# RWKV's small products on the undivided TensorE array, with a re-ordered start and end, in a hybrid decode step

## Chip, cores and metric

The kernel runs on one core of a Trainium2 chip. The metric is the device time of one execution in microseconds (us), taken as the median of several runs. PE is TensorE (matmuls; PEld its weight loads), DVE is VectorE, ACT is ScalarE, POOL is GpSimd, SP issues the DMAs.

## What is computed

One decoder layer over T = 304 tokens: 16 meta tokens and a prompt of 256, and 8 sequences of 4 sampled tokens. Two head groups stand side by side: RWKV-7 (16 heads of 64) and retention (4 heads of 256). Cut to what matters:

```python
xn = rms_norm(x, norm_mix); z = xn @ w_in            # 2048 -> 3360 + 4096 columns
z_a, z_b = z[..., :RWKV_COLS], z[..., RWKV_COLS:]
zs = z_a + mu * (z_prev - z_a)                        # token shift; then r, k, v, decay, a, gate
# rwkv7_scan, per token and head (S is 64x64):
sa = S @ a_t
S = S * w_t + outer(sa, b_t) + outer(v_t, k_t)
out_t = S @ r_t
# retention: (q k^T * decay mask) v, and a 256x256 state for each head
h = x + concat(o_a, o_b) @ w_out
h = h + (silu(hn @ w_gate) * (hn @ w_up)) @ w_down    # hn = rms_norm(h), d_ff = 5632
y = rms_norm(h, norm_final)                           # and all the states
```

## The kernel before

**Main stream.** All weights lie in HBM as one stream in the order in which they are used. `Step.main` takes them in tiles of up to 128 output columns; a tile of the input projection is 16 blocks of 128 rows. `load` brings 1,024 columns by DMA (`wr`), `halve` splits 512 of them into a rounded part on ACT (`wh`) and the rest on DVE (`wl`), and each block takes three matmuls (`xh,wh`, `xl,wh`, `xh,wl`) in fp32r into an accumulator `acc` in PSUM. Two accumulators take turns. `evacuate` scales the finished tile by 1/rms (`rstd1`); while that is not known, ACT copies the raw accumulator away so that the next tile may go on.

**Small products.** Eight pairs of RWKV heads (two heads of 64 = 128 partitions), each a generator `pair` with `by_token`, `inverse`, `units` and `sample`, work in five units of up to 64 tokens. Four retention heads follow in `ret`. Their matmuls are plain fp32, go to PSUM tiles named `mm`, and read tiles of one scratch arena (`arena_dt.float`). In the pairs most have 64 rows or 64 columns: the two heads stand in the two halves of the array, so products run two at a time on a divided array. `pairmm` is one of these, and the loop of `units` issues them step by step, with an ACT copy between two steps.

**Order.** A planner (`Plan`) writes the order of each engine while the kernel is built: it books a duration for each instruction, and as soon as no generator is ready by its clock, it lets the main stream emit one block. A generator's step that is about to use a divided array yields `DIV`; `Plan.pick` holds such a step back until the array is divided already, two of them wait, or `HOLD` = 2000 ns are over. Each engine's queue is then followed in order on the chip.

**Start.** `start` loads x in five chunks with halves of the weight tiles between, converts all 16 blocks (`xh` on ACT, `xl` on DVE), and `constants` squares x, adds the squares up on POOL, and sums over partitions with eight matmuls against a tile of ones (`ssq`).

**End.** The last tiles of the down projection add into `ht`; ACT squares, DVE adds to `ssq3`, `rstd_from` sums with three matmuls against ones, computes 1/rms on DVE and spreads it with three more matmuls; eight multiplies and DMAs end the kernel.

Of the kernel before, what the change touches and what calls it, by code (L numbers as in the profile page):

```python
# [15 lines left out]
P = 128  # L16
D = 2048
KT = D // P
SEQ = 256
# [22 lines left out]
LATE = 20000  # L42
WR = 4
# [7 lines left out]
HOLD = 2000  # L51

DIV = "div"
# [15 lines left out]
for _n, _w in [("id", 128), ("blk", 128), ("mar", 128), ("i64", 64), ("lvl", 2 * 64), ("m16", 64), ("i16", 16), ("h16", 32), ("h32", 64), ("rst", TP),   # L69
               ("bm64", 8), ("bm128", 8), ("ks", 12), ("kss", 4), ("qs", 128), ("own", 256), ("sel", 32)]:  # L70
    CV[_n] = _o
    _o += _w
# [48 lines left out]

def extent(key):

    if key[0] == "down":
        return min(FSTEP, FT - key[1]), P
    return 8 if key[0] == "out" else KT, 32 if key == ("in", 2) else P


def constants():
# [9 lines left out]
    put("mar", np.concatenate([(s < t), (s <= t)], 1).astype(f))  # L139
    put("i64", (s == t).astype(f))  # L140
# [8 lines left out]
    put("h32", (s // 32 == q // 32).astype(f))  # L149
# [6 lines left out]
    put("bm64", ((r[:64, None] % 32) // 4 == np.arange(8)[None, :]).astype(f))  # L156
# [34 lines left out]
def pack(x_prompt, x_sample, state_shift, state_rwkv, state_ret, meta_tokens, norm_mix, w_in,  # L191
# [20 lines left out]
    for k in seq:  # L212
        m = pick[k[0]](*k[1:])
        n = math.prod(extent(k))
        big[:, at:at + n] = m.reshape(m.shape[0] // P, P, m.shape[1]).transpose(1, 0, 2).reshape(P, n)
        at += n
# [82 lines left out]
class Plan:  # L299
# [57 lines left out]
    def add(self, gen, rank, ready=None):  # L357
        self.made += 1
        self.streams.append([rank, self.made, self.clock["PE"] if ready is None else ready, gen, None])
# [12 lines left out]

    def step(self, s):
        self.ready, self.end = s[2], s[2]
        try:
            s[4] = next(s[3])
# [96 lines left out]
class Step:  # L473
# [79 lines left out]
    def main(self, jobs):  # L553
# [3 lines left out]
        for j in jobs:  # L557
            while self.live == ACC or j.need is not None and not j.need():
                yield False
            self.flush()  # L560
            if j.prep is not None:
                j.prep()
            K, m = extent(j.key)
            n = j.cols[1] - j.cols[0]
            acc = self.t([P, 512], "acc", pool=self.ap_)
            self.live += 1
            for k in range(K):
                o = at % 512
                if o == 0:
                    while self.loaded < min(total, at + WR * WCOLS):  # L570
                        self.load()
                    while self.halved < min(total, at + (WS - 1) * 512):
                        self.halve()
                    hi, lo = self.halves.pop(0)
                xh, xl = (v[:, j.cols[0]:j.cols[1]] for v in j.xs[k])
                self.pe.matmul(acc[:m, :n], hi[:, o:o + m], xh, start=k == 0, stop=False)
                self.pe.matmul(acc[:m, :n], hi[:, o:o + m], xl, start=False, stop=False)
                self.pe.matmul(acc[:m, :n], lo[:, o:o + m], xh, start=False, stop=k == K - 1)
                at += m
                if k < K - 1:  # L580
                    yield True
            self.plan.add(self.evacuate(j, acc), 0, self.plan.clock["PE"] + 250)
            yield True

    def evacuate(self, j, acc):

        if j.ready is not None and j.ready not in self.done:
# [4 lines left out]
            self.live -= 1  # L592
# [7 lines left out]
        self.live -= 1  # L600
# [1027 lines left out]
```

## Time and profile before

| what | value |
|---|---|
| runs | 1596.07, 1601.77, 1598.37 us; median 1598.37 |
| profiled execution | 1596.75 us by the clock, 1594.9 us span |
| PE busy | 1561.5 us (98%), 12336 matmul records |
| PEld / DVE / ACT / POOL busy | 94% / 71% / 52% / 11% |
| chain that ended last | PE `acc` 81%, PE `mm` 10%, DVE arena 2%, POOL arena 1%, waits for x by DMA 1% |
| DMA | 252.55 MB, mean 158 GB/s, 51.2% of the engines' time |

The span is cut by the program into: the start up to about 27 us, the input projection with all small products up to about 650 us, the output projection and the feed-forward part up to 1580 us, and the end. In the third stretch PE takes one `acc` matmul of 288 columns after the other, 133 ns apart. A row of a timeline gives the start in us, the duration, engine, line, operation, tiles, rows*columns of the weights and the output's shape; matmuls are pipelined, so a product's share of PE is read from start to start, not from its duration. An fp32 product appears as two matmul records, an fp32 transpose or an fp32r matmul as one. The line is always that of a helper, so one goes by tiles.

### The profile page before, as it was taken

How to read it: one execution, taken by the hardware profiler on the slowest of the kernel's cores; microseconds unless marked ns; L12 is line 12 of the kernel's file. 1: busy time of each engine (PE TensorE's matmuls, PEld its weight loads, DVE VectorE, ACT ScalarE, POOL GpSimd, SP SyncE). 2: the span in 40 equal slices, each digit the busy share in tenths (PEclk: the TensorE clock that was granted, in tenths of full speed). 3: DMA queues.
4: the chain of work that ended last, by engine and by line, in shares of the span. 5: the costliest groups of instructions: out<-in, count | busy, mean ns of one | idle time of the engine just before them, and what ended most of it. 6: DMA issues, size and time to landing. Idle time of an engine off the chain costs nothing.

```text
span 1594.9 us, 32785 instructions
## 1 busy us (share of the span) xinstructions
PE 1561.5 (98%) x12336; PEld 1492.1 (94%) x12336; DVE 1130.3 (71%) x2603; ACT 833.4 (52%) x1801; POOL 173.3 (11%) x507
## 2 busy tenths in 40 slices
PE   7999999999999999999999999999999999999996
PEld 6998889888998888999999999999999999999996
DVE  5978889887898687777565656566666656565657
ACT  4665666767575656455444444444444444444445
POOL 3343224413143000000000000000000000000000
PEclk9999999999999999999999999999999999999998
DMA  6444343334543456755555555555555555555553
GB/s 236 146 137 127 90 131 114 121 118 156 166 134 118 158 164 220 251 164 160 170 162 170 161 170 161 171 161 170 161 170 162 170 162 170 163 168 163 168 163 109
DMA packets 76142, 252.55 MB, mean 158 GB/s; under 512 B 9296, under 2 KB 14288, under 8 KB 75984
## 3 DMA queue, kind: packets, MB, share of 16 engines
q1 hardware_dynamic: 75984, 250.46, 51.2%
q8 instruction: 97, 1.59, 0.4%
q14 instruction: 61, 0.50, 0.1%
HBM read 236.14 MB, written 14.28 MB: 157 GB/s over the span
## 4 chain that ended last, share of the span: by engine, by line
PE 91%; DVE 3%; POOL 1%; issue 1%; DMA 1%; ACT 1%; SPq 0%; DVEq 0%; ACTq 0%; POOLq 0%
PE acc L294 81%; PE mm L294 10%; DVE arena_dt.float L294 2%; POOL arena_dt.float L294 1%; DVE wl L294 1%; DMA arena_dt.float<-xT 1%; ACT arena_dt.float L294 1%; DMA arena_dt.float<-s0r 1%; ACT wh L294 0%; DVE xl L294 0%; ACT arena_dt.float32r L294 0%; SPq L294 0%; ACT xh L294 0%; POOL shout L294 0%; DVE arena_dt.float32r L294 0%
## 5 line engine op out<-in xcount | busy, mean ns | idle before, releaser
L294 ACT CAST wh<-wr 128x512 fp32r<-128x512 f32 x826 | 510.6, 620 | 596.1 <-PE acc L294 554.8
L294 PE MATMUL acc<-xh,wh 128*128 128x288 f32 (+3 forms) x2608 | 799.2, 306 | 7.5 <-ACT wh L294 6.0
L294 PE MATMUL acc<-xh,wl 128*128 128x288 f32 (+3 forms) x2608 | 777.5, 298 | 1.0 <-DVE wl L294 0.9
L294 PE MATMUL acc<-xl,wh 128*128 128x288 f32 (+3 forms) x2608 | 775.6, 297 | 0.0
L294 DVE TENSOR_TENSOR wl<-wr,wh 128x512 fp32r<-128x512 f32 x826 | 570.4, 692 | 275.6 <-ACT wh L294 251.8
L294 PEld LDWEIGHTS acc<-xh,wh 128*128 128x128 f32 (+1 forms) x2608 | 492.8, 189 | 21.7 <-ACT wh L294 7.6
L294 PEld LDWEIGHTS acc<-xl,wh 128*128 128x128 f32 (+1 forms) x2608 | 494.4, 190 | 3.6 <-issue 0.3
L294 PEld LDWEIGHTS acc<-xh,wl 128*128 128x128 f32 (+1 forms) x2608 | 491.4, 188 | 3.7 <-DVE wl L294 2.4
L294 PE MATMUL acc<-arena_dt.float32r,wh 128*128 128x288 f32 x1408 | 282.3, 295 | 0.3 <-DVE arena_dt.float L294 0.3
L294 PEld LDWEIGHTS acc<-arena_dt.float32r,wh 128*128 128x128 f32 x1408 | 228.2, 190 | 0.8 <-DVE arena_dt.float L294 0.5
L294 PE MATMUL acc<-arena_dt.float32r,wl 128*128 128x288 f32 x704 | 209.6, 298 | 0.0
L294 DVE TENSOR_TENSOR arena_dt.float<-arena_dt.float 128x288 f32<-128x288 f32 (+8 forms) x470 | 150.9, 347 | 13.4 <-PE mm L294 7.7
L294 PE MATMUL mm<-arena_dt.float 64*64 64x64 f32 (+8 forms) x1984 | 141.0, 259 | 7.6 <-DVE arena_dt.float L294 4.3
L294 PEld LDWEIGHTS mm<-arena_dt.float 64*64 64x64 f32 (+4 forms) x1984 | 102.9, 142 | 44.7 <-issue 22.6
L294 DVE TENSOR_TENSOR arena_dt.float<-arena_dt.float,acc 128x288 f32<-128x288 f32 x208 | 94.3, 454 | 65.1 <-PE acc L294 61.7
L294 PEld LDWEIGHTS acc<-arena_dt.float32r,wl 128*128 128x128 f32 x704 | 132.4, 188 | 0.0
L294 ACT COPY arena_dt.float<-mm 128x64 f32<-128x64 f32 (+9 forms) x305 | 85.9, 288 | 61.7 <-PE mm L294 54.5
L294 POOL TENSOR_TENSOR arena_dt.float<-arena_dt.float 128x75 f32<-128x75 f32 (+15 forms) x244 | 93.2, 382 | 94.8 <-DVE arena_dt.float L294 61.3
L294 DVE TENSOR_TENSOR arena_dt.float<-acc,arena_dt.float 128x288 f32<-128x288 f32 (+3 forms) x183 | 73.4, 418 | 33.0 <-PE acc L294 32.4
L294 ACT ACTIVATE arena_dt.float<-arena_dt.float 128x288 f32<-128x288 f32 (+5 forms) x199 | 83.3, 424 | 24.4 <-DVE arena_dt.float L294 21.9
L294 POOL COPY arena_dt.float<-arena_dt.float 128x32 f32<-128x32 f32 (+5 forms) x123 | 45.5, 383 | 216.3 <-DVE arena_dt.float L294 94.8
L294 ACT COPY arena_dt.float<-arena_dt.float 64x16 f32<-64x16 f32 (+4 forms) x128 | 36.5, 313 | 20.0 <-DVE arena_dt.float L294 13.4
(55 smaller groups left out, 638.3 us busy)
## 6 DMA issues: line engine op xcount, KB each, us to landing
wr<-big SPq DMA_DIRECT2D x411, 512.0 KB, 3.6
arena_dt.float<-s0r SPq DMA_DIRECT2D x16, 512.0 KB, 4.4
out_rts<-arena_dt.float SPq DMA_DIRECT2D x16, 512.0 KB, 3.4
arena_dt.float<-xT SPq DMA_DIRECT2D x4, 576.0 KB, 5.4
out_y<-arena_dt.float SPq DMA_DIRECT2D x8, 288.0 KB, 2.4
arena_dt.float<-s0w SPq DMA_DIRECT2D x8, 256.0 KB, 2.7
arena_dt.float<-lora SPq DMA_DIRECT2D x16, 128.0 KB, 2.2
out_rws<-arena_dt.float SPq DMA_DIRECT2D x8, 256.0 KB, 2.7
```

The source lines that it names most:

```text
L294: return f(*a, **k)
```

## The change

1. Each pair's products use the whole array. Operands of two heads are put side by side or on a diagonal with zeros (`arp`, `bku`, `tn`, `yy`, `rh`, `bt`), so that one product of 128 rows and 128 weight columns takes the place of two to four smaller ones. The second level of `inverse` gets its operand by a DVE transpose of the first level's result and no longer by a third set of matmuls. `DIV`, `HOLD` and the choice in `Plan.pick` go.
2. `steps()` orders the weights so that the first two tiles take turns, block by block. `start` brings x one or two blocks at a time, `convert` makes `xh`, `xl` just ahead of the block, and the first tile accumulates in a spare `mm` tile.
3. Ten matmuls of ones with ones stand ahead of the first block (`WARM`), and twice four at the end (`BRIDGE`).
4. All four squares of x are ACT's (two were DVE's), the adds DVE's (they were POOL's), and one of eight `ssq` matmuls is left.
5. At the end DVE squares the last tile, and `rstd_from` adds that square by a second matmul in each column instead of a DVE add.

```diff
+WARM = 10
+BRIDGE = 4
-HOLD = 2000
-DIV = "div"
+def steps():
+    seq = sequence()
+    first = [(key, k) for k in range(KT) for key in seq[:2]]
+    return first + [(key, k) for key in seq[2:] for k in range(extent(key)[0])]
     def pick(self, now):
-        ready = [s for s in self.streams if s[2] <= now]
-        div = [s for s in ready if s[4]]
-        rest = [s for s in ready if not s[4]]
-        if div and (self.mode not in (None, (P, P)) or len(div) > 1 and not rest
-                    or now - min(s[2] for s in div) >= HOLD):
-            return div[0]
-        return rest[0] if rest else None
+        return next((s for s in self.streams if s[2] <= now), None)
     ...
     def start(self):
+        x = lambda a, b: self.sp.dma_start(xr[:, a:b], I["xT"][:, a:b, :])
+        x(0, 1)
+        self.sp.dma_start(self.pvt, I["pv"])
+        self.load(2)
+        for k in range(1, KT, 2):
+            x(k, min(k + 2, KT))
+            if k + 1 < KT:
+                self.load(2)
+        pt = self.ps()
+        for _ in range(WARM):
+            self.pe.matmul(pt[:, :P], self.ones, self.ones, start=True, stop=True)
     ...
     def constants(self):
-            self.pool.tensor_add(xr[:, g:g + 2], xr[:, g:g + 2], xr[:, g + 2:g + 4])
+            self.act.activation(xr[:, g:g + 4], xr[:, g:g + 4], AF.Square)
+            if g % 8:
+                self.dve.tensor_add(xr[:, g - 4:g], xr[:, g - 4:g], xr[:, g:g + 4])
-        for g in range(0, KT, 4):
-            for j in range(2):
-                self.pe.matmul(ssq[:, :T], self.ones, xr[:, g + j, :], start=g + j == 0, stop=g + j == 13)
+        self.pe.matmul(ssq[:, :T], self.ones, xr[:, 0, :], start=True, stop=True)
     ...
     def inverse(self, mt, other):
-                    pe.matmul(pt[h, u * 64:(u + 1) * 64], lhs[h, u, :], rhs[h, u, :], start=True, stop=True)
+                pe.matmul(pt[:, u * P:(u + 1) * P], two(ems[li], u), flat(tn, u), start=True, stop=True)
     ...
     def units(self, p, sc, bkt, sv, sav, tt, arp, dl, o, other):
-            for hi, h in enumerate(HALF):
-                pe.matmul(pt[h, :64], sc[:, hi, u, :64], sv[:, hi, u, :], start=True, stop=True)
+            pe.matmul(pt[:, :P], sc[:, u, 0].rearrange("p h c -> p (h c)"), flat(sv, u), start=True, stop=True)
-            for pt, h in zip(pts, HALF):
-                pe.matmul(pt[h, :64], tt[h, u, :], rh[h], start=True, stop=True)
-            yield
+            pe.matmul(pt[:, :P], two(tt, u), rh.rearrange("p h c -> p (h c)"), start=True, stop=True)
     ...
     def rstd_from(self, ssq, more=None):
+            if more is not None:
+                self.pe.matmul(ps[:n, c:c + 1], more[:, c * n:(c + 1) * n], self.ones[:, :1], start=False, stop=True)
+        if more is not None:
+            self.bridge()
```

Counted along the two programs, the pairs' products and the array's shape change like this (an fp32 product is one here, two records in the trace):

| weights rows*columns, columns moved | before | after |
|---|---|---|
| 64*64, 64 | 464 | 0 |
| 128*64, 64 | 224 | 0 |
| 64*128, 128 | 80 | 0 |
| 128*64, 20 | 64 | 0 |
| 64*64, 512, or 128*128, 512 | 16 | 8 |
| transposes: 64*128, 64 and 128*64, 128 and 128*128, 128 | 80 and 56 and 48 | 0 and 0 and 120 |
| 128*128, 256 | 40 | 72 |
| 128*128, 128 (without those of ones) | 0 | 256 |
| 128*128, 64 and 40 | 0 | 64 and 32 |
| fp32r of 312 columns: half height, full height | 16, 16 | 0, 32 |
| changes of the array's shape, all told | 353 | 12 |

The order on PE at the start, before: the first tile (`acc_144`) is finished, then come the products with ones (`mm_336`), then the second tile (`acc_209`).

```order
L294 MATMUL acc_144<-xh_72,wh_94 128x304
L294 MATMUL acc_144<-xl_73,wh_94 128x304
L294 MATMUL acc_144<-xh_72,wl_95 128x304
...
L294 MATMUL acc_144<-xl_73,wh_130 128x304
L294 MATMUL acc_144<-xh_72,wl_131 128x304
L294 MATMUL mm_336<-arena_dt.float_70,ones_75 128x304 x5
L294 MATMUL acc_209<-xh_72,wh_175 128x290
```

And now: ones first, then the first tile (`mm_111`) and the second (`acc_125`) in turns; the single product with ones for the sum of squares (`mm_390`) stands in the fourth tile.

```order
L300 MATMUL mm_100<-ones_75 128x128 x10
L300 MATMUL mm_111<-xh_72,wh_114 128x304
L300 MATMUL mm_111<-xl_73,wh_114 128x304
L300 MATMUL acc_125<-xh_72,wh_114 128x290
L300 MATMUL acc_125<-xl_73,wh_114 128x290
L300 MATMUL mm_111<-xh_72,wl_115 128x304
L300 MATMUL acc_125<-xh_72,wl_115 128x290
...
L300 MATMUL acc_357<-xh_72,wl_299 128x304
L300 MATMUL mm_390<-arena_dt.float_70,ones_75 128x304
L300 MATMUL acc_357<-xh_72,wh_298 128x304
```

The second tile has moved ahead of the end of the first, and the sum of squares from between the first two tiles to 70 matmuls behind them.

On PE in the first pairs, before (`mm_1646` and `mm_1665` are steps of two inverses, one row for each head and unit):

```order
L294 MATMUL acc_1604<-xh_72,wl_1560 128x288
L294 MATMUL mm_1646<-arena_dt.float_70 64x64
L294 MATMUL mm_1647<-arena_dt.float_70 64x64
...
L294 MATMUL mm_1660<-cst_140,arena_dt.float_70 64x128 x2
L294 MATMUL mm_1665<-arena_dt.float_70 64x64
L294 MATMUL mm_1666<-arena_dt.float_70 64x64
...
L294 MATMUL acc_1604<-xh_72,wh_1559 128x288
```

And now (`mm_1602` and `mm_1631` are steps of one inverse, `mm_1640` transposes of `by_token`):

```order
L300 MATMUL acc_1590<-xh_72,wl_1527 128x288
L300 MATMUL mm_1602<-arena_dt.float_70 128x128 x4
L300 MATMUL acc_1590<-xh_72,wh_1526 128x288
...
L300 MATMUL acc_1590<-xh_72,wl_1557 128x288
L300 MATMUL mm_1631<-arena_dt.float_70 128x64 x4
L300 MATMUL mm_1640<-cst_262,arena_dt.float_70 128x128 x3
L300 MATMUL acc_1590<-xh_72,wh_1556 128x288
```

Steps of several pairs that stood together in one group are now apart, each between matmuls of the main stream: 185 groups of `mm` products have become 242.

On PE at the end, before (`mm_19529` sums over partitions, `mm_19542` spreads 1/rms):

```order
L294 MATMUL acc_19485<-arena_dt.float32r,wl_19445 128x288
...
L294 MATMUL acc_19506<-arena_dt.float32r,wh_19465 128x288 x2
L294 MATMUL acc_19506<-arena_dt.float32r,wl_19466 128x288
L294 MATMUL mm_19529<-ones_75,arena_dt.float_70 96x1 x3
L294 MATMUL mm_19542<-cst_140,arena_dt.float_70 128x96 x3
```

And now (`mm_18946` and `mm_18960` are the products of ones):

```order
L300 MATMUL acc_18627<-arena_dt.float32r,wl_18589 128x288
L300 MATMUL mm_18946<-ones_75 128x128 x2
L300 MATMUL acc_18645<-arena_dt.float32r,wh_18611 128x288 x2
...
L300 MATMUL mm_18953<-ones_75,arena_dt.float_70 96x1
L300 MATMUL mm_18960<-ones_75 128x128 x3
L300 MATMUL mm_18953<-ones_75,arena_dt.float_70 96x1 x5
L300 MATMUL mm_18960<-ones_75 128x128
L300 MATMUL mm_18974<-cst_262,arena_dt.float_70 128x96 x3
```

Two of the first four products of ones stand before the last tiles, the others among the last sums.

## Rows read from the trace of the kernel before

**Rows 1.** The page, part 1: engine, busy us, share of span, instructions.
```profile
PE 1561.5 (98%) x12336; PEld 1492.1 (94%) x12336; DVE 1130.3 (71%) x2603; ACT 833.4 (52%) x1801; POOL 173.3 (11%) x507
```

**Rows 2.** Groups by shape on PE, whole span: busy us, mean ns, idle before.
```profile
L294 PE MATMUL mm<-arena_dt.float 64*64 64x64 f32 x928 | 43.9, 226 | 3.7 <-DVE arena_dt.float L294 2.8 <-ACT arena_dt.float L294 1.0
L294 PE MATMUL mm<-arena_dt.float 128*64 128x64 f32 x448 | 30.9, 239 | 0.4 <-ACT arena_dt.float L294 0.4
L294 PE MATMUL mm<-arena_dt.float 64*128 64x128 f32 x160 | 13.8, 294 | 1.5 <-DVE arena_dt.float L294 1.5
L294 PE MATMUL mm<-arena_dt.float 128*64 128x20 f32 x128 | 8.5, 211 | 0.0
```

**Rows 3.** Timeline of PE about 208 us: a small group, then an undivided product.
```profile
207.71 0.30 PE L294 MATMUL acc<-xh,wl 128*128 128x290 f32 x1
207.94 0.33 PE L294 MATMUL mm<-arena_dt.float 64*64 64x64 f32 x4
...
208.44 0.29 PE L294 MATMUL acc<-xl,wh 128*128 128x290 f32 x1
...
208.98 0.30 PE L294 MATMUL acc<-xh,wl 128*128 128x290 f32 x1
209.12 0.65 PE L294 MATMUL mm<-arena_dt.float,cst 128*128 128x288 f32 x2
...
209.74 0.30 PE L294 MATMUL acc<-xl,wh 128*128 128x290 f32 x1
```

**Rows 4.** Timeline of PE about 219 us: a group of 20.
```profile
218.45 0.30 PE L294 MATMUL acc<-xh,wl 128*128 128x304 f32 x1
218.68 0.80 PE L294 MATMUL mm<-arena_dt.float 64*64 64x64 f32 x20
...
219.65 0.30 PE L294 MATMUL acc<-xl,wh 128*128 128x304 f32 x1
```

**Rows 5.** Timeline of PE about 382 us: undivided transposes of 128 columns.
```profile
382.19 0.30 PE L294 MATMUL acc<-xh,wl 128*128 128x290 f32 x1
382.33 0.60 PE L294 MATMUL mm<-cst,arena_dt.float 128*128 128x128 f32 x4
...
382.91 0.30 PE L294 MATMUL acc<-xl,wh 128*128 128x304 f32 x1
```

**Rows 6.** Timeline of all engines, the first 34 us.
```profile
7.92 1.87 ACT L294 ACTIVATE xh<-arena_dt.float,pv 128x304 fp32r<-128x304 f32 x4 [1.99 <-DMA arena_dt.float<-xT]
10.02 0.46 PE L294 MATMUL acc<-xl,wh 128*128 128x304 f32 x1
10.27 0.46 PE L294 MATMUL acc<-xh,wl 128*128 128x304 f32 x1
...
16.75 1.21 ACT L294 ACTIVATE arena_dt.float<-arena_dt.float 128x1216 f32<-128x1216 f32 x1
17.13 0.30 PE L294 MATMUL acc<-xh,wh 128*128 128x304 f32 x1
17.27 0.30 PE L294 MATMUL acc<-xl,wh 128*128 128x304 f32 x1
18.04 4.49 POOL L294 TENSOR_TENSOR arena_dt.float<-arena_dt.float 128x608 f32<-128x608 f32 x1 [1.84 <-ACT arena_dt.float L294]
22.57 1.29 PE L294 MATMUL mm<-arena_dt.float,ones 128*128 128x304 f32 x4 [2.35 <-POOL arena_dt.float L294]
33.94 0.30 PE L294 MATMUL acc<-xh,wh 128*32 128x290 f32 x1
```

**Rows 7.** The page, part 5: the split of the weights on ACT.
```profile
L294 ACT CAST wh<-wr 128x512 fp32r<-128x512 f32 x826 | 510.6, 620 | 596.1 <-PE acc L294 554.8
```

**Rows 8.** Waits of PE from 27 to 655 us, the largest: us in total, times, longest.
```profile
PE mm L294 <- DVE arena_dt.float L294: 4.5, 3, 2.8
```

**Rows 9.** Windows: length, busy us of PE, PEld, DVE, ACT, POOL (count), granted clock, DMA.
```profile
10.00:12.00 2.00, 2.00 (x8) 1.78 (x8) 1.13 (x3) 2.00 (x4) 0.51 (x1) 1.00 1.00 391
200.00:300.00 100.00, 99.57 (x892) 89.24 (x892) 90.46 (x273) 68.69 (x184) 34.05 (x107) 1.00 0.42 126
```

More of the change, by code (lines that the diff above doesn't have):

```diff
@@ L211, in pack @@
     at = 0
[L212 to L216, printed above, removed]
+    mats = {}
+    for key, k in steps():
+        if k == 0:
+            mats[key] = pick[key[0]](*key[1:])
+        m = mats[key][k * P:(k + 1) * P]
+        big[:, at:at + m.shape[1]] = m
+        at += m.shape[1]
     out["big"] = ca(big.reshape(P, -1, WCOLS).transpose(1, 0, 2))
@@ L556, in main @@
         at = 0
[L557 to L563, printed above, removed]
-            n = j.cols[1] - j.cols[0]
[L565 to L582, printed above, removed]
@@ new lines, in main @@
+        accs = {}
+        for key, k in steps():
+            j = jobs[key]
+            K, m = extent(key)
+            n = j.cols[1] - j.cols[0]
+            if k == 0:
+                while self.live == ACC or j.need is not None and not j.need():
+                    yield False
+                self.flush()
+                if j.prep is not None:
+                    j.prep()
+                if at:
+                    accs[key] = self.t([P, 512], "acc", pool=self.ap_)
+                    self.live += 1
+                else:
+                    accs[key] = self.first = self.ps()
+            acc = accs[key]
+            o = at % 512
+            if o == 0:
+                starting = self.converted < KT
+                self.convert(k + 1)
+                while self.loaded < min(total, at + WR * WCOLS):
+                    self.load()
+                while self.halved < min(total, at + (1 if starting else WS - 1) * 512):
+                    self.halve()
+                hi, lo = self.halves.pop(0)
+            self.convert(k + 3)
+            xh, xl = (v[:, j.cols[0]:j.cols[1]] for v in j.xs[k])
+            self.pe.matmul(acc[:m, :n], hi[:, o:o + m], xh, start=k == 0, stop=False)
+            self.pe.matmul(acc[:m, :n], hi[:, o:o + m], xl, start=False, stop=False)
+            self.pe.matmul(acc[:m, :n], lo[:, o:o + m], xh, start=False, stop=k == K - 1)
+            at += m
+            if k == K - 1:
+                del accs[key]
+                self.plan.add(self.evacuate(j, acc), 0, self.plan.clock["PE"] + 250)
@@ L591, in evacuate @@
             self.act.copy(raw[:m], acc[:m, :n])
-            self.live -= 1
+            self.live -= acc is not self.first
             yield
@@ L599, in evacuate @@
         more = next(post, self) is not self
-        self.live -= 1
+        self.live -= acc is not self.first
         if more:
@@ new lines, in pair @@
+        pool.memset(v0, 0.0)
+        act.copy(bku[:, 0].rearrange("p (q c) -> p q c", q=2)[:, :, :META], bk[:, :, :META])
+        act.copy(v0[:, 1, :META], v[:, :META])
+        units = lambda a: a[..., META:NP].rearrange("p q (u c) -> p u q c", c=64)
+        for hi, h in enumerate(HALF):
+            act.copy(arp[h, 0, 0, hi, :META], ra[h, 0, :META])
+            act.copy(arp[h, 1:, :, hi], units(ra[h]))
+        act.copy(bku[:, 1:].rearrange("p u (q c) -> p u q c", q=2), units(bk))
+        yield
@@ L1083, in units @@
[L1083 to L1092 removed]
+                nxt = st[h] if u == NU - 1 else sv[h, u + 1, hi, :]
@@ L1458, in rstd_from, with bridge @@
         return ps[:, :TO]
+    def bridge(self):
+        pt = self.ps()
+        for _ in range(BRIDGE):
+            self.pe.matmul(pt[:, :P], self.ones, self.ones, start=True, stop=True)
     def out_jobs(self, half):
@@ L1578, in build @@
         self.start()
-        self.plan.add(self.constants(), 0)
-        self.plan.run(self.main([jobs[k] for k in sequence()]))
+        self.plan.run(self.main(jobs))
         self.sp.dma_start(self.O["sh"], self.shout)
```

331 lines of the change are left out of this document (166 added, 165 removed).

## Prediction

> **What bounds the kernel now.** I read the page's busy shares first: PE is busy for 98% of the span and its weight loads for 94% [rows 1], so a gain must come out of PE's own sequence. The waits say the same of the stretch with the small products: between 27 and 655 us PE waited in 14 places for 9.7 us in all, the largest sort being the one shown [rows 8]. Everything between two main-stream matmuls there is therefore paid by PE itself, and it is the small products. To price them I left the durations alone, since a record of a 64*64 product shows a mean of 226 ns [rows 2] while twenty of them pass in less than a microsecond [rows 4]; I read from start to start instead. Last I read the first 34 us engine by engine [rows 6], where PE waits and runs slowly, and the windows for DVE, the busiest engine behind PE [rows 9].
>
> **The prices.** Main-stream matmuls of 304 columns follow each other by 0.14 us [rows 6], those of 288 and 290 by 0.134 in proportion. The span from the last of them before a group to the second one after it, less two such steps, is what the group costs. Four records of 64*64: 208.44 - 207.71 - 0.27 = 0.46 us [rows 3]. Twenty: 219.65 - 218.45 - 0.28 = 0.92 us [rows 4]. The difference gives 0.0285 us for a record and leaves 0.35 us, that is 0.175 us for each of the two changes of the array's shape, in and out. An fp32 product of 288 columns on the whole array costs 209.74 - 208.98 - 0.27 = 0.49 us, 0.247 a record, and nothing beside it: twice 288 columns at 2.4 columns a nanosecond are 0.240 [rows 3]. Four transposes of 128 columns: 382.91 - 382.19 - 0.27 = 0.45 us, 0.112 a record [rows 5], again two passes of the columns and no more, although each loads its own 128 weight columns.
>
> The granted clock enters as a level: those prices are at the upper level of 2.4 GHz. In the first 17 us main-stream matmuls follow each other by 0.25 us [rows 6], the pace of 1.2 GHz, and the windows print 1.00 there all the same [rows 9]; I go by the intervals.
>
> **1. Small products, the largest term.** What goes, with counts from the rows where they stand there and else from the table of the change: 928 and 448 records by 0.0285 are 26.4 and 12.8 us; 160 records with twice the columns, by 0.057, are 9.1; 128 records of 20 columns [rows 2] lie between 0.0285 and 0.057, and I take the upper, 7.3, since the weights to be loaded are as wide; the transposes, 80 by 0.0285 and 56 by 0.057, are 5.5. Together 61.1 us. The changes of shape fall from 353 to 12: 341 by 0.175 are 59.7 us. Gone: 120.8 us. What comes: 32 products of 256 columns by 0.43 are 13.8; 256 of 128 columns, two records each, by 0.224 are 57.3; 96 of 64 or 40 columns, which no row shows on the whole array, cost between their columns alone (9 us for all) and the 0.112 a record that 128 weight columns and 128 moved ones took; I take the second, 21.5, because the weights are the same width. 72 transposes by 0.112 are 8.1, and the 16 fp32r products that lose their half-height partner 1.1. Coming: 101.8 us. The products of 512 columns cancel (four passes of 512, eight times, for two at a time, sixteen times). Net: 19 us less, between 15 (if 20 columns cost 0.0285) and 31 (columns alone).
>
> The rule that speaks against this is in the Trainium skill, "TensorEngine Tiling (Array Packing)", Theoretical Speedup: dividing the array for sizes of 64 or less is worth up to a factor of two in each dimension, and giving it up should cost that. The trace agrees for the products themselves (61.1 us divided, 101.8 undivided), and that alone would make the kernel slower; the sum turns only on the 59.7 us of shape changes. The same page, Key Properties, says that changing the shape drains the array, without a price; the price above is the trace's.
>
> The pairs' work on the other engines hardly changes: counted along the programs, DVE has 2470 instructions for 2483, ACT 1793 for 1799. POOL gets some 60 more clearings of small tiles and loses its four adds of squares; it fills 34 us of 100 [rows 9] and the clearings wait for nobody's result, so I cost them at nothing, covered by its idle two thirds.
>
> **2. The start.** Before, the third tile begins at 33.94 us, after a wait for POOL (an add of 4.49 us, then PE idle for 2.35 before the products with ones) [rows 6]. Now two limits stand for the first two tiles. ACT: 16 conversions by 0.47 (four take 1.87), eight splits by 0.62 [rows 7], two squares by 1.21 [rows 6], 14.9 us from the landing of the first block, which I put at 3.5 us, so it ends at 18.4; DVE's last halves, the final products and the third tile's weights behind another square bring the third tile to 20.5 to 21.5. PE: ten products of ones, twenty records of two passes of 128 columns at the lower level, 4.3 us, end at about 5.4 and lie under the wait for data. Then 96 matmuls take 13.4 us at the upper level (end at 18.8) or 24 at the lower (end at 29.4). I take 21.5, near the ACT limit. Gain 12.4 us, between 4.5 and 14. SP issues 18 transfers for x and the first weights instead of 9, and the rotation table, shift and constants now stand behind them and three weight tiles; their first readers follow the sum of squares, so nobody should notice. That sum itself now waits for DVE and stands 70 matmuls into the third and fourth tile, some 10 us behind the last conversion, while ACT and DVE need about 6 for it; the finished tiles meanwhile leave by raw copies of ACT, as the first did before.
>
> **3. New waits.** The held-back steps had slack; now each is issued as soon as the planner thinks it ready, and 185 groups become 242. At the old rate, 9.7 us in some 150 groups, 57 more cost 3 us (0 to 10). What is queued behind a late group is the main stream itself.
>
> **4. The end.** One ACT square and one DVE add leave the last chain; six of eight ones products lie in front of its matmuls, and the order shows two already among the last tiles. I take 0, within 1 us either way.
>
> Sum: -19.0 - 12.4 + 3 = -28.4 us. Against the profiled execution, 1596.75 us (span 1594.9), that is 1568.3; that execution lies 1.6 us below the median of the runs shown, 1598.37, so for the median **1570 us**.
>
> **Rivals.**
> - *Forecast* (chance 0.66): as above, 1556 to 1580.
> - *The clock stays at the lower level through the first two tiles* (0.11). Before, the pace was the lower one still at 10.27 us and the upper one at 17.13 [rows 6]. In the changed kernel the third tile would start at 29.4: 1578. The Trainium skill, "TensorE: Matmul & The Clock Gate", Part 1, has the lower level as the default that activity lifts; by it the ones would have lifted it before the data come, and the sum would be 2.7 us better, with the two tiles ended at 18.8.
> - *DVE becomes the bound* (0.07). It fills 90.5 of 100 us between 200 and 300 [rows 9]. 19 us less in 620 raises that to 93: tight, not full. If it lost a third of the 19 us in the dense stretches: 1576.
> - *The start is not kept* (0.06). 1/rms is known no sooner than before, so the pairs start no sooner, and the main stream, 12 us ahead, stops at the third pair's tiles, which wait for the first pair. Eleven tiles by 6.6 us lie in front of that, so I doubt it. 1582.
> - *Both of the last two, or little of the array's gain* (0.03): 1590 to 1598, no change that counts. About 0.3%, 5 us, is what a measurement can tell.
> - *Slower: waits in place of shape changes* (0.05). A group that is issued too early stops PE, whose queue is in order, with the whole main stream behind it. A wait was 0.7 us on average (9.7 in 14). Without waits the gain is 31.4 us; 45 more such waits, in every fourth of the pairs' groups, eat it, and in every second group they would give 1630. For it: each of the 15 steps of `units` in a pair is now alone between main-stream matmuls with an ACT copy before it. Against it: groups that were never held back wait seldom now [rows 8].
> - *Slower: the shape changes do not pay* (0.02). If the 0.175 us belonged to small fp32 products among fp32r ones and not to the shape, 61 us of work become 102 and the rest stays: 1598 + 40.7 - 12.4 + 3 = 1630. Against it: the 288-column product costs nothing beside its passes [rows 3].
>
> **How the numbers follow.** Likeliest 1570. Range 1556 to 1587: the lower end has half of the doubt in the narrow products, the upper end takes in the clock, DVE and the start, and leaves some 10% above. Faster 0.90, same 0.03, slower 0.07.
>
> **What would show it.** Right: `mm` groups of 128*128 in the pairs that cost 0.22 us a product with no 0.35 beside it; the third tile's first matmul (32 weight columns) at 20 to 22 us; PE's waits in the middle at 10 to 15 us; DVE at 85 to 92% there; the feed-forward stretch untouched. Wrong: 0.25 us steps beyond 12 us; waits on `mm` of 30 us and more; products of 64 or 40 columns far off 0.22 us; a main stream that pauses before the third pair.

## The result, and the profile after

The changed kernel takes 1582.05 us (median of 4 runs, 1580.62 to 1583.19) against 1598.83 (4 runs, 1596.07 to 1601.77): ratio 0.9902, 95% interval 0.9885 to 0.9919. Faster by 1.0% and within the range, but by 15.7 us (by the ratio) where 28.4 were forecast. The profiled executions differ by 14.1 us (spans 1594.9 and 1580.8).

The page after, part 1, answers to [rows 1]: nearly 1000 matmul records less on PE, the same busy share.

```profile
PE 1544.1 (98%) x11388; PEld 1510.5 (96%) x11388; DVE 1125.7 (71%) x2590; ACT 842.7 (53%) x1795; POOL 182.5 (12%) x567
```

The timeline of PE at three places: the start (answers to [rows 6]), the first product behind the output projection, and the last tile. Columns as there.

```profile
1.05 4.63 PE L300 MATMUL mm<-ones 128*128 128x128 f32 x20 [1.05 <-DVE ones L300]
5.86 0.62 PE L300 MATMUL mm<-xh,wh 128*128 128x304 f32 x1 [0.17 <-ACT wh L300]
...
7.17 0.31 PE L300 MATMUL mm<-xh,wh 128*128 128x304 f32 x1
7.31 0.30 PE L300 MATMUL acc<-xh,wh 128*128 128x290 f32 x1
...
22.46 0.30 PE L300 MATMUL acc<-xh,wh 128*32 128x290 f32 x1
...
731.93 0.33 PE L300 MATMUL mm<-ones,arena_dt.float 128*96 128x1 f32 x3
...
1566.64 0.29 PE L300 MATMUL acc<-arena_dt.float32r,wl 128*128 128x288 f32 x1
```

And the same two later places before:

```profile
742.02 0.34 PE L294 MATMUL mm<-ones,arena_dt.float 128*96 128x1 f32 x3
...
1579.72 0.29 PE L294 MATMUL acc<-arena_dt.float32r,wl 128*128 128x288 f32 x1
```

These starts cut the span into four stretches:

| stretch | before, us | after, us | change | forecast |
|---|---|---|---|---|
| start, up to the third tile | 33.9 | 22.5 | -11.5 | -12.4 |
| middle, from there to the first 128*96 product | 708.1 | 709.5 | +1.4 | -16.0 (-19.0 and +3) |
| feed-forward, to the last tile's last matmul | 837.7 | 834.7 | -3.0 | 0 |
| end | 15.2 | 14.2 | -1.1 | 0 |

So the start came as forecast, and the middle, where 19 us of products were to go, gave nothing. Two views say why. First PE's waits in the middle (us in total, times, longest); they answer to [rows 8]:

```profile
PE mm L300 <- DVE arena_dt.float L300: 10.6, 9, 2.6
PE mm L300 <- ACT arena_dt.float L300: 9.8, 5, 3.8
PE mm L300 <- POOL arena_dt.float L300: 0.8, 1, 0.8
PE acc L300 <- DVE wl L300: 0.7, 1, 0.7
PE mm L300 <- DMA arena_dt.float<-s0r: 0.4, 1, 0.4
```

With two small groups more that is 22.8 us in 19 waits; before, the same stretch had 10.8 in 15. The waits are not many more but longer: six of 1.8 to 3.8 us. Second, the windows of 4 us behind some of these (columns as in [rows 9]):

```profile
120.00:124.00 4.00, 3.97 (x18) 4.00 (x19) 2.47 (x7) 0.90 (x2) 0.00 (x0) 0.50 0.43 118
124.00:128.00 4.00, 4.00 (x26) 4.00 (x25) 2.48 (x12) 1.44 (x4) 1.04 (x5) 0.73 0.03 13
312.00:316.00 4.00, 4.00 (x25) 4.00 (x25) 3.28 (x9) 1.10 (x2) 0.55 (x2) 0.76 0.12 36
368.00:372.00 4.00, 2.98 (x12) 2.62 (x12) 2.26 (x10) 1.52 (x6) 0.21 (x3) 0.57 0.48 134
504.00:508.00 4.00, 3.28 (x30) 1.68 (x34) 1.35 (x11) 1.05 (x3) 3.02 (x13) 0.63 0.18 70
```

PE waited 3.80 us until 120.03, then did 18 records in 4 us at a granted clock of 0.50, the lower level of 1.2 GHz, and came back to the upper one by 128. Such a wait is paid twice. Over the middle, windows of 4 us times (1 - clock) add up to 8.6 us after and 3.4 before; I call this the clock's loss below. In all kernels here it comes in steps of some 1.7 us, two before and five after. It is read from one execution, and executions differ in it: the six of life40 below took from 1578.39 us at a mean granted clock of 0.997 to 1588.05 at 0.991.

What is left of the middle without waits and clock's loss is PE's own work: 708.1 - 10.8 - 3.4 = 693.9 before, 709.5 - 22.8 - 8.6 = 678.1 after. So PE's own work there did become cheaper, by some 16 us, and 17.2 us more of waits and slow clock ate it.

DVE did not become full; between 200 and 300 us it is busy for less than in [rows 9]:

```profile
200.00:300.00 100.00, 98.48 (x706) 94.76 (x706) 87.61 (x266) 70.06 (x177) 38.45 (x114) 1.00 0.42 132
```

**One long wait, followed back.** The timeline of all engines before 185.84 us:

```profile
182.80 3.62 POOL L300 TENSOR_TENSOR arena_dt.float<-arena_dt.float 128x30 f32<-128x30 f32 x12
...
184.96 0.01 DVE L300 LOAD_MASK_SELECT arena_dt.float<-arena_dt.float  x1 [2.36 <-POOL arena_dt.float L300]
184.96 0.24 DVE L300 STREAM_SHUFFLE arena_dt.float<-arena_dt.float 128x80 f32<-128x80 f32 x1
185.11 0.59 DVE L300 SCALAR_TENSOR_TENSOR arena_dt.float<-mm,arena_dt.float 64x64 f32<-64x64 f32 x2
...
185.84 0.46 PE L300 MATMUL mm<-arena_dt.float 128*128 128x128 f32 x2 [2.65 <-DVE arena_dt.float L300]
```

PE needs the two DVE operations of one pair's `units`. They read a product that PE had done by 183.2 us, where its wait begins, but DVE works in order, and ahead of them stands a shuffle of another pair's `inverse`, which may not start while POOL is behind in its loop of 15 steps. The planner books such a step of POOL (100 ns and 2.2 ns per element) at 0.17 us or less; these 12, one behind the other, took 0.30 us each. The same picture, ACT or DVE stopped for POOL and PE's step behind it, stands before 120.03 and 369.02:

```profile
118.69 0.56 ACT L300 ACTIVATE arena_dt.float<-arena_dt.float,pv 128x312 f32<-128x312 f32 x1 [3.03 <-POOL arena_dt.float L300]
...
120.03 1.30 PE L300 MATMUL mm<-arena_dt.float 128*128 128x64 f32 x5 [3.80 <-ACT arena_dt.float L300]
```

```profile
367.78 0.01 DVE L300 LOAD_MASK_SELECT arena_dt.float<-arena_dt.float  x1 [2.12 <-POOL arena_dt.float L300]
...
369.02 0.77 PE L300 MATMUL mm<-arena_dt.float 128*128 128x128 f32 x2 [2.58 <-DVE arena_dt.float L300]
```

Before 504.72 it stands with shorter stops (ACT 0.65 us). Before 309.51 DVE works without a pause on what PE waits for, and before 461.98 a chain of DVE and ACT steps ends late, so POOL has a part in four of the six.

### The profile page after: what moved, and what is told of

It reads as the page before. It is cut to its first block, busy times and chain, and to the rows that moved or that the text cites. A ratio compares the mean times of both kernels' runs of the same rounds, so it can differ in the third digit from the quotient of the medians.

```text
span 1580.8 us, 30987 instructions
## 1 busy us (share of the span) xinstructions
PE 1544.1 (98%) x11388; PEld 1510.5 (96%) x11388; DVE 1125.7 (71%) x2590; ACT 842.7 (53%) x1795; POOL 182.5 (12%) x567
## 4 chain that ended last, share of the span: by engine, by line
PE 68%; ACT 1%; DVE 1%; DMA 0%; issue 0%; POOL 0%; DVEq 0%; ACTq 0%; POOLq 0%
PE acc L300 64%; PE mm L300 4%; ACT arena_dt.float L300 1%; DVE arena_dt.float L300 1%; DMA arena_dt.float<-s0r 0%; DVE wl L300 0%; ACT wh L300 0%; ACT arena_dt.float32r L300 0%; POOL arena_dt.float L300 0%; DVEq L1672 0%; DVE arena_dt.float32r L300 0%; ACTq L300 0%; DVEq L300 0%; POOLq L300 0%
## 5 line engine op out<-in xcount | busy, mean ns | idle before, releaser
L300 PE MATMUL acc<-xh,wh 128*128 128x288 f32 (+2 forms) x2592 | 791.8, 305 | 0.5 <-ACT wh L300 0.3
L300 PE MATMUL acc<-xh,wl 128*128 128x288 f32 (+2 forms) x2592 | 771.3, 298 | 0.7 <-DVE wl L300 0.7
L300 PE MATMUL acc<-xl,wh 128*128 128x288 f32 (+2 forms) x2592 | 768.1, 296 | 0.0
L300 PEld LDWEIGHTS acc<-xh,wh 128*128 128x128 f32 x2592 | 488.3, 188 | 6.4 <-issue 2.7
L300 PEld LDWEIGHTS acc<-xl,wh 128*128 128x128 f32 x2592 | 487.5, 188 | 4.6 <-issue 1.4
L300 PEld LDWEIGHTS acc<-xh,wl 128*128 128x128 f32 x2592 | 486.9, 188 | 1.7 <-DVE wl L300 1.2
L300 PE MATMUL mm<-arena_dt.float 128*128 128x128 f32 (+8 forms) x1072 | 171.9, 320 | 19.3 <-DVE arena_dt.float L300 10.6
L300 PEld LDWEIGHTS mm<-arena_dt.float 128*128 128x128 f32 (+1 forms) x1072 | 140.2, 185 | 36.9 <-issue 10.5
L300 DVE TENSOR_TENSOR arena_dt.float<-arena_dt.float 128x288 f32<-128x288 f32 (+10 forms) x483 | 157.3, 351 | 11.1 <-ACT arena_dt.float L300 4.4
L300 ACT COPY arena_dt.float<-mm 64x64 f32<-64x64 f32 (+9 forms) x330 | 92.4, 287 | 53.0 <-PE mm L300 48.1
L300 ACT ACTIVATE arena_dt.float<-arena_dt.float 128x288 f32<-128x288 f32 (+6 forms) x200 | 85.3, 432 | 33.8 <-DVE arena_dt.float L300 28.0
(64 smaller groups left out, 680.7 us busy)
```

What stands on the lines that cost most here:

```text
L300: return f(*a, **k)
```

## The experiments

All ratios are to the kernel before, measured on the same chip, except for prices, which ran once. Each kernel has one trace. "The changed kernel" was measured by itself (0.9902), so differences to it are best taken between ratios. Where an expectation speaks of waits of over 0.15 us, it counts a wait from start to start over the price of its group, which takes in part of the slow clock: 10.7 us before, 32.7 after. No single view prints that count; where given, it stands in parentheses behind the waits by the rows (10.8 and 22.8).

### The two halves apart

start_alone has the new `steps`, `start`, `convert`, `main` and `constants` in the kernel before; products_alone has the undivided products there, and no `DIV`. From each, two lines of the change:

```diff
+    first = [(key, k) for k in range(KT) for key in seq[:2]]
+            self.convert(k + 3)
```

```diff
+            pe.matmul(pt[:, :P], two(tt, u), rh.rearrange("p h c -> p (h c)"), start=True, stop=True)
+        return next((s for s in self.streams if s[2] <= now), None)
```

> The kernel before with the new start alone (first two tiles in turns, conversion block by block, ten products of ones ahead, squares on ACT, one product for the sum of squares); small products, hold-back rule and end are those of before. Theory (start's gain is kept): the third tile (32 weight columns) begins at 22 to 23 us instead of 33.9 and all the rest follows 11 to 12 us earlier: ratio to before 0.9925 to 0.9935, about 1587 us. Rival (1/rms and the pairs start no sooner, so the main stream stops later for them): third tile at 22 to 23 us, but PE's waits between 27 and 740 us grow by 5 us or more, and the time is 1592 to 1598.

Measured: 1586.91 us, 0.9930 (0.9915 to 0.9945). The third tile starts at 22.25 us, the middle takes 711.6 with 12.6 us of waits (14.7). The start's gain is kept but for 3.5 us, waits and clock's loss; the rival falls.

> The kernel before with the undivided products alone (and no hold-back rule); start and end are those of before. Theory (the price of the products is as forecast, and the waits that eat the gain come with the undivided products): products and shape changes 20 to 22 us cheaper, PE's waits of over 0.15 us in the middle 20 us or more longer than the 10.7 us of before, time 1592 to 1598. Rival (the waits come from the early start, which lets the pairs' work crowd): waits stay near 10 us, and the time falls by about 19 us to 1579.

Measured: 1594.96 us, 0.9976 (0.9966 to 0.9987). Waits 23.5 us (31.6), clock's loss 8.5: the waits come with the products, not with the early start. By the ratios the two halves give 11.2 and 3.8 us, together near the whole's 15.7.

### The prices by themselves

```diff
+            if key[0] in ("gate", "up") and key[1] >= 12 and k in (3, 7, 11):
+                self.trial(TRIALS[(2 * key[1] + (key[0] == "up")) % len(TRIALS)])
```

> The changed kernel with groups of products of ones between the main stream's matmuls of the feed-forward part, three in each gate and up tile from the 13th on, of eight kinds in turn; nobody reads them. What a group costs is read from start to start. By the prices of the prediction: four undivided products of 128 columns 0.90 us (four of one 0.224), one of them 0.22; four of 64 columns 0.90 by the value taken (the weights set it), 0.43 by the columns alone; four of 32 columns 0.90 or 0.21; two products of 64*64 with 64 columns 0.35 + 4 times 0.0285 = 0.46, eight of them 0.35 + 16 times 0.0285 = 0.81; four of 128*64 with 64 columns 0.58; four of 64*64 with 16 columns 0.58 or less. Rival (0.175 us belongs to small fp32 products and not to the shape): the undivided group of one product costs 0.35 us more than 0.22.

Timeline of PE, two of the kinds with the main stream around them:

```profile
1000.93 0.29 PE L302 MATMUL acc<-xh,wl 128*128 128x288 f32 x1
1001.16 0.68 PE L302 MATMUL mm<-ones 64*64 64x64 f32 x16
1001.77 0.40 PE L302 MATMUL acc<-xh,wh 128*128 128x288 f32 x1
1002.01 0.30 PE L302 MATMUL acc<-xl,wh 128*128 128x288 f32 x1
...
1071.65 0.29 PE L302 MATMUL acc<-xh,wl 128*128 128x288 f32 x1
1071.78 0.97 PE L302 MATMUL mm<-ones 128*128 128x32 f32 x8
1072.59 0.38 PE L302 MATMUL acc<-xh,wh 128*128 128x288 f32 x1
1072.81 0.30 PE L302 MATMUL acc<-xl,wh 128*128 128x288 f32 x1
```

Eight products of 64*64: 1002.01 - 1000.93 - 0.27 = 0.81 us, as forecast; two took 0.46. Four undivided ones of 32 columns: 1072.81 - 1071.65 - 0.27 = 0.89, and those of 64 and of 128 columns took 0.895 as well, one of 128 columns 0.221. Four of 128*64 took 0.58. So the prices of the prediction hold to 0.01 us, the taken 0.224 for narrow products with them, and the 0.175 us belongs to the change of shape: the undivided group has nothing of it.

### POOL's late loop: booked too short, or places reused too early?

pool_cost books POOL by the trace; the others give the scratch arena's places another life, with the order unchanged.

```diff
-            dur = fixed + per * n
+            dur = fixed + per * n
+            if eng == "POOL":
+                dur = 100 + 0.85 * n if what == "memset" else 240 + 2.6 * n
```

> The changed kernel; the planner books POOL's instructions with durations near those of the trace (240 ns + 2.6 ns per element in place of 100 + 2.2; clearings 100 + 0.85), nothing else. Theory (new waits come because POOL's 15-step loop in inverse is booked too short, so DVE's and ACT's instructions that wait for POOL are queued too early, and the PE step behind them too): PE's waits of over 0.15 us in the middle fall from 32.7 us to 8 to 18, time 1564 to 1572. Rival (DVE, 88% busy in the dense stretches, is the cause and POOL only goes along with it): waits stay at 25 us or more, time 1579 to 1585. Second rival (pairs take longer by the new booking, and the main stream has to wait for them): slower, 1585 to 1600.

Measured: 1579.15 us, 0.9882 (0.9864 to 0.9899): some 3 us less than the changed kernel, with intervals that overlap, and waits at 23.2 us (34.5). The first theory falls: the waits only moved. What fell is the clock's loss, to 3.4. Time and count are where the rival has them, which does not yet show DVE as the cause.

```diff
-            b += slack
+            b += slack + 160 * late
```

`late` is 1 where the last reader is POOL; life40 has 40 for 160, and life0 no such term and a `slack` of 0.

> The changed kernel; a place in the arena whose last reader is POOL stays taken for 160 booked instructions more (some 10 us) before another tile may have it; for the room, weights have three buffers in place of four. The order on the engines stays. Theory (new waits come from reuse: ACT and DVE, in order, stand at an instruction that writes a place which POOL's late loop still reads, and the step that PE needs stands behind it): PE's waits of over 0.15 us between the third tile and the output projection fall from 32.7 us to 10 to 18, DVE's waits for POOL from 15.8 to under 8, time 1562 to 1571. Rival (they wait for POOL's results): waits stay at 28 us or more, time 1578 to 1584. Second rival (three buffers are too few): PE's waits of acc for wh and wl grow by 5 us or more, slower.

> As life160 with 40 booked instructions more (some 2.5 us) and four weight buffers. Theory (reuse): between the changed kernel and life160, PE's waits 18 to 26 us, time 1569 to 1577. Rival (POOL's results): waits stay at 28 us or more, time 1578 to 1584.

> The changed kernel; every place in the arena may be taken again right behind its last reader (the changed kernel leaves 10 booked instructions between). Theory (reuse): more of the writes meet a reader that is late; PE's waits rise from 32.7 us to 38 to 50, time 1587 to 1600. Rival (POOL's results): waits within 4 us of 32.7, time 1579 to 1585.

Measured: life160 1580.88 us, 0.9897 (0.9884 to 0.9910); life40 1582.57, 0.9909 (0.9891 to 0.9926); life0 1590.32, 0.9954 (0.9942 to 0.9966). In the middle 704.1, 709.5 and 716.3 us against 709.5. Shorter lives cost 7 us, longer ones gave 5 there (and a slower pace in the feed-forward part took 4 back, below). Waits: 21.7 (28.5), 22.9 (29.9) and 28.5 us (37.0). The time of life0 is the theory's, its count lies just below the theory's band; time and count of life40 and life160 are the rival's, and DVE's waits for POOL in life160 are 13.6 us, not under 8. Reuse is a part of it, not the whole.

```diff
+        rss = self.t([P, 3, NU, 16], "rss")
-            rs = self.t([P, NU, 16], "rs")
+            rs = rss[:, s % 3]
```

> The changed kernel; the 15 shuffles of inverse write three places of their own in turn (rs) in place of a tile of the arena each, so that a shuffle waits at most for the POOL product three steps earlier; the order of the instructions stays. Theory (the longest new waits begin where DVE, in order, stands at a shuffle that may not yet overwrite what POOL reads): DVE's waits for POOL fall from 15.8 us to under 6, PE's waits in the middle from 32.7 to about 22, time 1572 to 1577. Rival (what is late is POOL's result, not its reading): DVE's waits move to the next reader of the result, PE's waits stay within 4 us, time 1580 to 1584.

Measured: 1596.55 us, 0.9993 (0.9982 to 1.0004), slower than the changed kernel by 14 us. My edit did the opposite of what it was for. In the changed kernel each of the 15 shuffles has a tile of its own; three places in turn tie DVE to POOL more tightly. DVE's waits for POOL (us in total, times, longest) after, in own_rs3, and before:

```profile
DVE arena_dt.float L300 <- POOL arena_dt.float L300: 15.8, 21, 2.4
```

```profile
DVE arena_dt.float L300 <- POOL arena_dt.float L300: 28.3, 53, 1.8
```

```profile
DVE arena_dt.float L294 <- POOL arena_dt.float L294: 19.5, 47, 1.3
```

PE's waits went to 33.8 us (43.4) and the clock's loss to 13.6. It fits the picture at 185.84: DVE stopped longer for POOL, and PE with it. But the total of DVE's stops does not decide by itself: before, it was larger than after, and PE waited half as long.

pool_both joins pool_cost and life160.

> The changed kernel with pool_cost and life160 together (POOL booked by the trace; its places kept for 160 booked instructions more, the others for 20; three weight buffers). Theory (two separate causes, a result of POOL that is late and a place that is not yet free): what the two gave in the middle adds up, 2.6 and 5.4 us, time 1572 to 1577, PE's waits under 24 us. Rival (one cause seen twice): 1578 to 1582, waits at 26 us or more.

Measured: 1581.73 us, 0.9907 (0.9892 to 0.9922), middle 706.3, waits 22.7 (31.1). Time and count are the rival's: what the two gave does not add up. I took from it that neither is *the* cause, and looked for something that lets any error in the bookings show.

### The cover that went with the shape changes

`Plan.array` books 90 ns for a change of the array's shape; the trace shows 175. In the kernel before, 349 changes in the middle would make PE arrive 30 us later than planned, spread over the stretch, which gives each late engine time (I call this time the cover). before_175 takes this cover from the kernel before; pe97 gives the changed kernel one, pe104 (1.04 in place of 0.97) takes more away.

```diff
-            self.mode, self.parts, self.empty = mode, {}, self.clock["PE"] + 90
+            self.mode, self.parts, self.empty = mode, {}, self.clock["PE"] + 175
```

```diff
+        dur *= 0.97
         at = max(self.parts.get(part, self.empty), self.ready, self.begun + 5)
```

> The kernel before; its planner books 175 ns for a change of the array's shape, as the trace shows it, in place of 90. Theory (the hidden cover: 349 changes that took 85 ns longer than booked, 30 us in all, made PE arrive later than planned and so gave DVE, ACT and POOL, whose instructions are booked too short, the time they needed; without that cover they are late): PE's waits of over 0.15 us between third tile and output projection rise from 10.7 us to 25 to 35, time 1610 to 1622. Rival (the cover was the holding back of steps, which is still there): waits stay at 8 to 15 us, time 1593 to 1602.

Measured: 1620.5 us, 1.0148 (1.0132 to 1.0163). Booking the truth makes the kernel before 23 us slower. PE's waits in its middle are 20.3 us in 18 (24.9), the three largest sorts being

```profile
PE mm L294 <- DVE arena_dt.float L294: 5.3, 3, 2.9
PE mm L294 <- ACT arena_dt.float L294: 5.3, 6, 2.7
PE mm L294 <- POOL arena_dt.float L294: 5.2, 4, 2.4
```

and the clock's loss is 10.3 us. The middle is 21.0 us longer: 9.5 of waits, 6.9 of clock, and 4.6 of work, about the price of 30 more shape changes (the order groups fewer divided steps), 5.3. Another 4 us lie in the start, which I did not follow up. The time is in the theory's band, the count just under it. The rival, that holding back was the cover, falls: the rule was still there. The booking is the only thing that changes: tiles of the arena are free right behind their last reader in the kernel before too.

> The changed kernel; the planner books PE's instructions at 0.97 of their durations, so that PE arrives later than planned, by 20 us in 700, as it did before; three weight buffers, for the room in the arena that the longer lives want (places 16 booked instructions free in place of 10). Theory (lost cover): PE's waits fall from 32.7 us to 10 to 18, time 1564 to 1573. Rival (the waits are chains and full engines, which no cover helps): waits stay at 26 us or more, time 1576 to 1585.

Measured: 1570.60 us, 0.9839 (0.9823 to 0.9855), the fastest of all. That it is the time forecast for the change is chance: it still has 7.4 us more of waits and clock's loss than before. Middle 701.5 us, waits 18.2 (30.8), clock's loss 3.4. The two largest sorts of PE's waits:

```profile
PE mm L300 <- DVE arena_dt.float L300: 10.0, 11, 2.2
PE mm L300 <- ACT arena_dt.float L300: 6.1, 8, 1.8
```

The time is in the theory's band; the waits, 4.6 us less by the rows, are not: by the count of the expectation they are the rival's. The larger part of the middle's gain is the clock, 5.2 us, since the waits that are left are shorter (none over 2.2 us). Three weight buffers and longer lives of places are hardly what helped: life160 (longer lives behind POOL) and pool_both (20 instructions everywhere, more behind POOL, and POOL booked by the trace) have both and take 9 and 11 us more by the ratios. pe97's own lives of 16 with the old booking were not run.

> The changed kernel; the planner books PE's instructions at 1.04 of their durations, so that PE arrives earlier than planned, by some 26 us in 700; four weight buffers and places free after 10 booked instructions, as in the changed kernel. Theory (cover): the opposite of pe97. PE's waits, 22.7 us by the rows of the waits in the changed kernel, rise to 32 to 50 us, the stretches at a clock below 1.00 that follow long waits get more, time 1592 to 1606. Rival (any other order gives another time, up or down, and pe97 was a lucky one): time 1572 to 1590, waits within 6 us of 22.7.

Measured: 1591.44 us, 0.9964 (0.9952 to 0.9976). Middle 717.2, waits 26.5, clock's loss 11.9. The two largest sorts of PE's waits:

```profile
PE mm L300 <- DVE arena_dt.float L300: 13.7, 15, 3.0
PE mm L300 <- ACT arena_dt.float L300: 4.6, 7, 2.7
```

The direction is the theory's, the size below it: the time falls between the two bands, the waits are in the rival's. In the middle the three bookings 0.97, 1 and 1.04 give 701.5, 709.5 and 717.2, the order that the theory asks for. With one kernel for each booking this does not rule out that another order by itself moves the time by some us.

All kernels together, us; work is the middle less waits and clock's loss:

| kernel | time | middle | PE's waits | clock's loss | work |
|---|---|---|---|---|---|
| before | 1598.8 | 708.1 | 10.8 | 3.4 | 693.9 |
| start_alone | 1586.9 | 711.6 | 12.6 | 5.1 | 693.9 |
| before_175 | 1620.5 | 729.1 | 20.3 | 10.3 | 698.5 |
| products_alone | 1595.0 | 710.1 | 23.5 | 8.5 | 678.1 |
| changed | 1582.1 | 709.5 | 22.8 | 8.6 | 678.1 |
| pool_cost | 1579.2 | 706.9 | 23.2 | 3.4 | 680.3 |
| life160 | 1580.9 | 704.1 | 21.7 | 1.7 | 680.7 |
| life40 | 1582.6 | 709.5 | 22.9 | 6.8 | 679.8 |
| life0 | 1590.3 | 716.3 | 28.5 | 5.1 | 682.7 |
| own_rs3 | 1596.6 | 723.9 | 33.8 | 13.6 | 676.5 |
| pool_both | 1581.7 | 706.3 | 22.7 | 5.1 | 678.5 |
| pe97 | 1570.6 | 701.5 | 18.2 | 3.4 | 679.9 |
| pe104 | 1591.4 | 717.2 | 26.5 | 11.9 | 678.8 |

The last column falls into two kinds, divided near 694 to 699 and undivided at 676 to 683. Most of what else moved the time of the middle is waits and clock.

How large the cover is can be counted along the programs. The planner's own clock for PE, read while a kernel is built, gives the middle 665.6 us before and 665.6 after: by its bookings the change saves nothing there. The cover is the work less this planned time, and the last column here is waits and clock's loss together, us:

| kernel | planned middle | cover | waits and clock |
|---|---|---|---|
| pe97 | 647.2 | 32.7 | 21.6 |
| before | 665.6 | 28.3 | 14.2 |
| changed | 665.6 | 12.5 | 31.4 |
| before_175 | 699.5 | -1.0 | 30.6 |
| pe104 | 692.2 | -13.4 | 38.4 |

Within the divided kernels and within the undivided ones, less cover goes with more waits and clock's loss. But pe97, with as much cover as the kernel before, keeps 7.4 us more: cover goes with some 10 of the 17.2 us.

## Why the prediction was right and where it failed

**1. Small products (-19.0).** Right in mechanism and nearly in size: the work fell by 15.8 us, inside 15 to 31, and the prices run confirms the prices it tried. The rule against the change, in the Trainium skill, "TensorEngine Tiling (Array Packing)", Theoretical Speedup (up to a factor of two for each small dimension), agrees with that run for the product alone: a 64*64 product costs (0.81 - 0.46) / 6 = 0.06 us divided and 0.224 undivided. The sum turned, as said, on the shape changes.

**2. The start (-12.4).** Measured -11.5 in place, -11.7 in start_alone. products_alone, which has the old start, begins its third tile at 32.95 us, so 1 us of this is no more than the spread between kernels. The upper pace came by 7 us, with 0.14 us from 7.17 to 7.31; the rival with the lower clock is out, and so is the one in which the start is not kept.

**3. New waits (+3, 0 to 10): the step that failed.** It said: at the old rate, 9.7 us in some 150 groups, 57 more cost 3 us. (With 150 groups that is 3.7; 3 comes out with the 185.) Measured +12.0 us of waits and +5.2 of clock behind them, 17.2 in all, outside the bounds. Two things were wrong in it. The old rate was not a property of groups but of a kernel whose PE had 28 us of cover; the change took 16 of them away, and I counted each 0.175 us as gain and none as cover. In before_175, taking the cover away brings 16.4 us of waits and clock by itself. And a wait was priced at its length only. The rival "waits in place of shape changes" had the mechanism and was weighed at 0.05; its price per wait (0.7 us) was too low and its number of waits too high.

A term of the first part stood at nothing too soon: POOL's clearings, "small tiles" that nobody waits for. Between 20 and 740 us POOL has 113 of them after, 28.5 us, and 50 before, 7.9 us; the costliest sorts after are

```profile
L300 POOL MEMSET arena_dt.float<- 64x512 f32 x16 | 8.5, 531 | 0.7 <-POOL arena_dt.float L300 0.2
L300 POOL MEMSET arena_dt.float<- 128x512 f32 x8 | 4.2, 525 | 3.1 <-PE mm L300 2.3 <-DVE arena_dt.float L300 0.9
```

Nobody need wait for a clearing itself, but POOL's loop stands behind it: one of 0.52 us begins at 365.72 us and one at 501.38, in front of two of the long waits. No run takes the clearings away, so their share is open. They are not the whole, since before_175 has as many as before and 30.6 us of waits and clock.

**4. The end (0, within 1).** -1.1, just outside. products_alone has the old end and takes 14.3 us there, so this is not shown to come from the new one.

**Not foreseen: the feed-forward part (-3.0).** It was forecast as untouched, and products_alone has it too (834.3 us). Its windows, before and after:

```profile
800.00:1100.00 300.00, 300.00 (x2261) 300.00 (x2260) 185.22 (x316) 128.54 (x220) 0.00 (x0) 1.00 0.55 166
```

```profile
800.00:1100.00 300.00, 300.00 (x2270) 300.00 (x2269) 185.08 (x314) 129.31 (x221) 0.00 (x0) 1.00 0.55 166
```

No wait, no lower clock, the same matmuls, 0.4% more of them in the same time. 0.4% of 838 us is the 3 us; the last section returns to it. Some 2 to 3 us of the middle's 15.8 may be the same.

The sum: -11.5 + 1.4 - 3.0 - 1.1 = -14.2 us against -28.4. Waits and clock miss by 14.2, products by 3.2, start by 0.9; feed-forward and end give 4.1 back. Those 4.1 us are luck: without them the time would be some 1586 us, just inside the range.

What stays open is how the 12 us of waits divide among POOL's bookings and clearings, reuse of places and DVE's own backlog, as before 309.51 us. In pool_both, mending two of them together gave no more than either.

## What to carry to other kernels

Where a planner fixes each engine's order, compare its bookings with the trace before removing anything that is booked too cheaply: what it takes beyond its booking can be a cover that other engines live on. If it goes, try booking that engine a little too short; here 3%, with three weight buffers and longer lives of places, went with some 10 us. Price a wait with what follows it, and look at the long waits one by one, not only at their sum.

## What the hardware showed that was not expected

- **The clock behind a wait.** Of the six long waits after, those of 3.80, 1.83, 2.58 and 2.28 us have windows with a granted clock of 0.50 to 0.81 at their end or behind it; those of 2.65 and 2.95 (until 185.84 and 461.98) have none. Length alone does not decide, and the cost does not follow it: a wait of 4.8 us in life160 cost one step of 1.7 us, that of 3.80 two. The Trainium skill, "TensorE: Matmul & The Clock Gate", Part 1, has pauses of the engine bring back the lower level; the trace agrees in kind.
- **Narrow undivided fp32 products cost no less.** 32, 64 and 128 columns all take 0.224 us; on the divided array four of 64*64 with 16 columns took 0.53 us, of which the two shape changes are 0.35.
- **The pace of an unchanged stream differs between kernels.** In 300 us of the feed-forward part PE did 2261 records before, 2270 after, 2272 in pe97, 2264 in own_rs3, 2259 in life160 and 2258 in pe104, at clock 1.00 and without waits: 0.6% from end to end, up to 5 us of the time. These kernels differ there in where their tiles lie; I did not try that by itself, so the cause is open.
